# Eleven weight blocks that a matrix engine read as plain FP32 are split in two halves, and one tile's searches move

## The chip, the cores and the metric

The kernel runs on one core of a Trainium2 chip. The core has a matrix engine (TensorE, in the profile PE, with PEld for its weight loads), three engines for elementwise work (VectorE or DVE, ScalarE or ACT, GpSimd or POOL) and SyncE (SP), which issues most of the DMA transfers. Each engine executes its own list of instructions in order, and waits on semaphores for the others. The metric is the device time of one execution in microseconds; lower is better.

## The reference, cut to what matters

One layer of a streaming encoder on 512 tokens of width 1024: a normed and modulated mixer (short convolution and a gated linear recurrence), and then a retrieval layer over 16384 single-neuron experts. Nearly all of the time is in the retrieval, and the change is there:

```python
h = modulate(rmsnorm(x, norm2_g[l]), sh2, sc2)
x = x + g2[:, None, :] * peer(h, w_q[l], sub_keys[l], expert_u[l], expert_v[l])
...
q = (xb @ w_q).reshape(p, PEER_HEADS, 2, PEER_DK_HALF)
sc = jnp.einsum('phcd,hcnd->phcn', q, sub_keys)          # two rows of 128 scores per head
top_s, top_i = lax.top_k(sc, PEER_TOPK)                  # 16 best of each
cand_s = (top_s[:, :, 0, :, None] + top_s[:, :, 1, None, :]).reshape(p, PEER_HEADS, kk)
best_s, best_pos = lax.top_k(cand_s, PEER_TOPK)          # 16 best of 256 pairs
idx = jnp.take_along_axis(cand_i, best_pos, axis=-1)
g = jax.nn.softmax(best_s, axis=-1)
act = jax.nn.gelu(jnp.einsum('phkd,pd->phk', expert_u[idx], xb), approximate=False)
return jnp.einsum('phk,phkd->pd', g * act, expert_v[idx])
```

## The kernel before, in words

The tokens stand in four tiles of 128. For the first tile and for 64 tokens of the second the kernel gathers the experts' rows and takes products token by token (the sparse way: 192 products with rows of `expert_u`, called dots, 128 weighted sums with rows of `expert_v`; GpSimd issues a gather of 512 KB for each). For the other 320 tokens it computes all 16384 activations as matrix products, in 128 blocks of 128 experts (the dense way).

In order of time: the adaLN vectors, the mixer, its output projection; then

- **the norm stretch** (205 to 235 us): the second norm. For each of eight slices of the width VectorE scales, ScalarE writes the upper part of the modulated input (L364), VectorE the rest of it (L365). The upper and lower parts `h2h` and `h2l` together carry the FP32 value. L674 writes it a third time, unsplit, to `h2f`, for the 320 dense tokens.
- **the query phase** (to 279 us): for each of eight heads one block of `w_q` is split and multiplied, transposed queries are copied (`qT`, L728), multiplied by the keys, and the scores are copied to `sc` (L738). VectorE searches the scores meanwhile. One step of the search (`top16`, L690 to L699) takes one head and one tile of tokens: the best eight of each of two rows of 128, their places, a copy without them, and the next eight. The generator `early` lists the steps that are done here, `HQ` heads with four tiles each. At its end the activations of block 0 are computed (L740).
- **the activation phase** (to about 770 us): blocks 1 to 123 of activations, with the weights streamed from HBM. `w_load` starts the load of a block, `w_high` lets ScalarE write the upper part of the weights (`whi`, L74) and `w_low` lets VectorE write the rest (`wlo`, L79). A split block takes 24 matmuls (`mm3`, L88 to L90): upper by upper, upper by lower, lower by upper. ScalarE then evicts the block through a gelu (L1150).
- **the second phase** (to about 1310 us): the dense products with `expert_v`, 18 matmuls of 128x512 for each of 128 blocks (L1349), the other activation blocks, the sums of the sparse way (L1083), and the output.

Blocks 1 to 11 are an exception in the kernel before (`k < FN`, FN = 12). They aren't split: their raw FP32 weights are multiplied by `h2f` in eight FP32 matmuls (L1159), of two records each in the trace. From block 5 on the raw weights are loaded to the buffers of `whi` and `wlo`; those of blocks 1 to 4 to `wraw`. Each of the three rings has four buffers.

What sets the order around the change: in the query phase the order of the program and a scheduler that places each engine's instructions; from block 0 on an order written by the loop at L1278. For each block k it issues the low half of block k+2, the matmuls, and the high half of block k+3, and then lets generators hand out VectorE's other work: `searches_E` (the rest of the searches that the second tile needs, then its final top 16 and positions in `topk_tile`), `rest_E` (the remaining searches), `gates_E` (the dense gates), `dots`. How much is handed out for a block is counted in nanoseconds by `pe`, `dve` and `ac`: a block adds its estimated TensorE time to `pe`, and VectorE's work is issued until `dve` has caught up. As soon as the second tile's positions are known (`idx_b`, L835), GpSimd's gathers open (L1045).

Names in the profile: `ps_act` and `ps_z` are sums in PSUM, `act` evicted activations, `h` the split input, `rows` gathered rows, `oh` one-hot or pair tables, `cl` and `ch` the split coefficients of the second phase. `in_uT_dram` and `in_v_dram` are the weights.

Of the kernel before, what the change touches and what calls it, by code (L numbers as in the profile page):

```python
# [34 lines left out]
def block_kernel(ctx, tc, xT, small, w_ada1, w_ada, b_ada, w_in, w_r, w_i, w_out, w_q, keys, uT, u, v, final_g, out):  # L35
# [618 lines left out]
    h2f = [ring.tile([128, 2, NU], F32, name="act", bufs=RB // 2) for _ in range(KB // 2)]  # L654
# [12 lines left out]
    for k in range(KB):  # L667
        if k == 2:
            qsp[1] = split_w(qraw[1])
            norm2.close()  # L670
        t1 = sq_pool.tile([128, T], F32, name="mt1")
        nc.vector.tensor_mul(t1, xs[:, k, :], psr2)
        modulate(t1, k, A2, adac[:, 24:32], h2h, h2l, full2)
        nc.scalar.activation(h2f[k // 2][:, k % 2], t1[:, T - NU:], AF.Identity, scale=A2[:, k:k + 1],  # L674
                             bias=adac[:, 24 + k:25 + k])
        if k < len(x1p):
            x1_out(*x1p[k])
# [30 lines left out]

    early = chain(*(stage1([h], range(NT)) for h in range(HQ)))

# [68 lines left out]
    def topk_tile(t):  # L779
# [30 lines left out]
        for w in range(2):  # L810
# [5 lines left out]
            if t == 1 and w == 0:  # L816
                yield None
# [146 lines left out]
    def searches_E():  # L964
        heads = range(HQ, 8)
        yield from stage1(heads, [1])
# [133 lines left out]
    def w_load(k):  # L1100
        if k < len(jobs):
            kind, i = jobs[k]
            if 5 <= k < FN:
                raw = wring.tile([128, KB, 128], FR, name=("wlo", "whi")[k % 2], bufs=WB).bitcast(F32)
                nc.sync.dma_start(raw, uT[i])
                wraw[k] = raw
                return
# [8 lines left out]
    def w_high(k):  # L1116
        if FN <= k < len(jobs):
            whi[k] = high(wraw[k])

    def w_low(k):  # L1120
        if FN <= k < len(jobs):
            wlo[k] = low(wraw.pop(k), whi[k])
            settle()
# [28 lines left out]
    def u_chunk(k, pool):  # L1152
        c = jobs[k][1]
        if c:
            ps = pool.tile([128, NU], F32, name="ps_act", bufs=3 if pool is psE else 2)
            if k < FN:
                raw = wraw.pop(k)
                for j in range(KB):
                    nc.tensor.matmul(ps, raw[:, j, :], h2f[j // 2][:, j % 2], start=j == 0, stop=j == KB - 1)  # L1159
            else:  # L1160
                mm3(ps, whi.pop(k), wlo.pop(k), hd, ld, range(KB), True, True)
# [5 lines left out]
        pe[0] += FPE if c and k < FN else 3530  # L1167
        dve[0] += 0 if c and k < FN - 2 else 1140
        ac[0] += 450 if c and k < FN - 3 else 1400
# [75 lines left out]
    pe, dve, ac = [0], [-HEAD], [0]  # L1245
# [32 lines left out]
    for k in range(CE):  # L1278
# [13 lines left out]
        dve[0] = max(dve[0], RHO * pe[0] - LEAD - (HEAD if k < 9 else 0))  # L1292
# [157 lines left out]
FN = 12  # L1450
DX = 0.3
FPE = 4400
# [6 lines left out]
HEAD = 0  # L1459
# [15 lines left out]
HQ = 5  # L1475
# [49 lines left out]
```

## Time and profile before

| | |
|---|---|
| median of 3 runs | 1326.58 us (1324.27 to 1328.68) |
| the profiled execution | 1323.76 us |
| its span on the core | 1321.9 us |
| TensorE busy | 1302.3 us |
| VectorE busy | 1209.9 us |
| ScalarE busy | 729.0 us |
| GpSimd busy | 505.8 us |
| mean DMA rate | 333 GB/s |

The profiled execution lies at the lower end of the three runs. A row of the timeline gives start, duration, engine, line, operation, what it writes and reads, how many instructions it joins, and in brackets the idle time ahead of it with what ended that. A row of a group of instructions gives busy time, the mean of one in ns, and the idle time ahead. A row of a stretch gives start and end, then TensorE, weight loads, VectorE, ScalarE and GpSimd with busy us and number of instructions, the granted TensorE clock, the DMA engines' busy share, and GB/s.

### The profile page before, as it was taken

How to read it: one execution, taken by the hardware profiler on the slowest of the kernel's cores; microseconds unless marked ns; L12 is line 12 of the kernel's file. 1: busy time of each engine (PE TensorE's matmuls, PEld its weight loads, DVE VectorE, ACT ScalarE, POOL GpSimd, SP SyncE). 2: the span in 40 equal slices, each digit the busy share in tenths (PEclk: the TensorE clock that was granted, in tenths of full speed). 3: DMA queues.
4: the chain of work that ended last, by engine and by line, in shares of the span. 5: the costliest groups of instructions: out<-in, count | busy, mean ns of one | idle time of the engine just before them, and what ended most of it. 6: DMA issues, size and time to landing. Idle time of an engine off the chain costs nothing.

```text
span 1321.9 us, 21365 instructions
## 1 busy us (share of the span) xinstructions
PE 1302.3 (99%) x7506; PEld 1127.4 (85%) x7506; DVE 1209.9 (92%) x2241; ACT 729.0 (55%) x1319; POOL 505.8 (38%) x342
## 2 busy tenths in 40 slices
PE   8999999999999999999999999999999999999996
PEld 6677777777999999999999998888888888888884
DVE  6889975899999999999999679999899999999998
ACT  4577736424785987799679543334343434343433
POOL 0000002300253126324655545677556555455560
PEclk9999999999999999999999999999999999999998
DMA  9765542342899999999999999999999999999993
GB/s 373 268 245 175 182 137 96 117 153 75 297 377 353 318 343 399 418 357 341 417 408 416 401 354 381 413 413 416 412 415 413 414 413 415 412 414 412 407 394 153
DMA packets 151276, 440.06 MB, mean 333 GB/s; under 512 B 17024, under 2 KB 44672, under 8 KB 151168
## 3 DMA queue, kind: packets, MB, share of 16 engines
q1 hardware_dynamic: 104016, 267.23, 54.3%
q0 software_dynamic: 46864, 170.41, 32.4%
q8 instruction: 59, 0.97, 0.3%
q10 hardware_dynamic: 288, 1.05, 0.2%
q14 instruction: 49, 0.40, 0.1%
HBM read 393.54 MB, written 45.09 MB: 332 GB/s over the span
## 4 chain that ended last, share of the span: by engine, by line
PE 74%; DMA 12%; DVE 9%; issue 3%; ACT 1%; DVEq 0%; SPq 0%; ACTq 0%
PE acc L1349 19%; PE ps_act L88 10%; PE ps_act L90 10%; PE ps_act L89 10%; DMA wraw<-in_v_dram 9%; PE ps_z L89 4%; PE ps_z L90 4%; PE ps_z L88 4%; PE ps_act L1159 4%; PE ps_gt L908 3%; DVE ys L1083 2%; DMA h<-Gd 2%; DVE wlo L79 1%; PE ps_z L346 1%; DMA raw<-in_v_dram 1%
## 5 line engine op out<-in xcount | busy, mean ns | idle before, releaser
L74 ACT ACTIVATE whi<-wraw 128x1024 fp32r<-128x1024 f32 x255 | 270.6, 1062 | 263.4 <-DMA wraw<-in_v_dram 176.0
L79 DVE TENSOR_TENSOR wlo<-wraw,whi 128x1024 fp32r<-128x1024 f32 x249 | 303.4, 1219 | 33.7 <-ACT whi L74 33.3
L88 PE MATMUL ps_act<-h,whi 128*128 128x320 f32 x928 | 291.8, 314 | 0.0
L89 PE MATMUL ps_act<-h,whi 128*128 128x320 f32 x928 | 287.1, 309 | 0.0
L90 PE MATMUL ps_act<-h,wlo 128*128 128x320 f32 x928 | 287.1, 309 | 0.0
L1045 POOL DMA_INDIRECT rows<-in_u_dram,idx_s x128 | 200.3, 1565 | 152.7 <-DVE scr L1066 106.5
L1045 POOL DMA_INDIRECT rows<-in_v_dram,idx_s x128 | 191.0, 1492 | 156.9 <-DVE ys L1083 134.9
L1349 PE MATMUL acc<-whi,cl 128*128 128x512 f32 x744 | 229.4, 390 | 0.0
L1349 PE MATMUL acc<-wlo,ch 128*128 128x512 f32 x744 | 229.3, 389 | 0.0
L1349 PE MATMUL acc<-whi,ch 128*128 128x512 f32 x744 | 229.2, 389 | 0.0
L1045 POOL DMA_INDIRECT rows<-in_u_dram,idx_b x64 | 94.0, 1469 | 212.2 <-DVE scr L1066 151.5
L88 PEld LDWEIGHTS ps_act<-h,whi 128*128 128x128 f32 x928 | 174.3, 188 | 0.5
L89 PEld LDWEIGHTS ps_act<-h,whi 128*128 128x128 f32 x928 | 174.5, 188 | 0.2
L90 PEld LDWEIGHTS ps_act<-h,wlo 128*128 128x128 f32 x928 | 174.3, 188 | 0.0
L1066 DVE SCALAR_TENSOR_TENSOR scr<-rows,h2n 128x1024 f16<-128x1024 f32 x128 | 156.4, 1222 | 12.3 <-DMA rows<-in_u_dram,idx_s 10.8
L1083 DVE SCALAR_TENSOR_TENSOR ys<-rows,acts,ys 128x1024 f32<-128x1024 f32 x127 | 163.6, 1288 | 1.5
L1349 PEld LDWEIGHTS acc<-whi,cl 128*128 128x128 f32 x744 | 139.6, 188 | 29.3 <-DVE cl L1240 0.3
L1349 PEld LDWEIGHTS acc<-wlo,ch 128*128 128x128 f32 x744 | 139.7, 188 | 29.0
L1349 PEld LDWEIGHTS acc<-whi,ch 128*128 128x128 f32 x744 | 139.5, 188 | 28.5
L1150 ACT ACTIVATE act<-ps_act 128x320 f32<-128x320 f32 x127 | 56.5, 445 | 108.3 <-PE ps_act L90 75.4
L896 ACT ACTIVATE igh<-oh,gl 128x128 f16<-128x128 f16 x320 | 99.6, 435 | 0.6 <-DVE oh L875 0.4
L595 POOL DMA_DIRECT2D x1d<-xn x8 | 4.6, 582 | 214.6 <-ACT xn L594 212.5
(326 smaller groups left out, 1933.1 us busy)
## 6 DMA issues: line engine op xcount, KB each, us to landing
wraw<-in_uT_dram SPq DMA_DIRECT2D x120, 512.0 KB, 7.2
wraw<-in_v_dram SPq DMA_DIRECT2D x103, 512.0 KB, 14.1
Gd<-stg SPq DMA_DIRECT2D x46, 512.0 KB, 8.9
wada<-in_w_ada_dram SPq DMA_DIRECT2D x45, 512.0 KB, 6.1
Ad<-act SPq DMA_DIRECT2D x48, 320.0 KB, 7.7
act<-Ad SPq DMA_DIRECT2D x48, 320.0 KB, 14.6
raw<-in_v_dram SPq DMA_DIRECT2D x25, 512.0 KB, 13.8
h<-Gd SPq DMA_DIRECT2D x48, 256.0 KB, 14.6
```

What stands on the lines that cost most here:

```text
L74: nc.scalar.activation(hi, raw, AF.Copy)
L79: (eng or nc.vector).tensor_sub(lo, raw, hi.bitcast(F32))
L88: nc.tensor.matmul(ps, hi[:, k, :], xh(k), start=first and k == ks[0], stop=False)
L89: nc.tensor.matmul(ps, hi[:, k, :], xl(k), start=False, stop=False)
L90: nc.tensor.matmul(ps, lo[:, k, :], xh(k), start=False, stop=last and k == ks[-1])
L896: nc.scalar.activation(ig[:, 1, k // 2, :, k % 2], of[:, k // 2, 0, :, k % 2], AF.Copy, scale=gl[:, t0 + k:t0 + k + 1])
L1045: nc.gpsimd.indirect_dma_start(out=r[:, :], out_offset=None, in_=table, in_offset=bass.IndirectOffsetOnAxis(ap=idxs[:, k:k + 1], axis=0))
L1066: nc.vector.scalar_tensor_tensor(scr, rows.pop(n), 1.0, hn, op0=OP.mult, op1=OP.mult, accum_out=dst[:, k:k + 1])
L1083: nc.vector.scalar_tensor_tensor(ys, rows.pop(k), acts[:, k:k + 1], ys, op0=OP.mult, op1=OP.add)
L1150: nc.scalar.activation(act[c // 2][:, c % 2], ps, AF.Gelu)
L1159: nc.tensor.matmul(ps, raw[:, j, :], h2f[j // 2][:, j % 2], start=j == 0, stop=j == KB - 1)
L1349: nc.tensor.matmul(accs[b][e], st[:, bs], mv[:, e * 512:(e + 1) * 512], start=first, stop=last)
```

## The change

`h2f` and L674 go. Blocks 1 to 11 are split like all others: `w_load` reads them to `wraw`, `w_high` splits every block, and `w_low` gives the low halves of blocks below PL = 10 to GpSimd, those of 10 and 11 to VectorE. The counters take 3530 ns for every block, and VectorE's counter adds nothing for blocks whose low half (two blocks ahead) is GpSimd's. `HQ` is 4 instead of 5, and `early` gets the second tile's (tile 1) searches of heads 4, 5 and 6 in addition: 16 + 3 = 19 steps instead of 20. Only head 7 of the second tile is left to `searches_E` (one step instead of three), and `rest_E` has twelve steps instead of nine. In `topk_tile` the second tile's second copy of positions is issued one block later.

```diff
-    h2f = [ring.tile([128, 2, NU], F32, name="act", bufs=RB // 2) for _ in range(KB // 2)]
...
         modulate(t1, k, A2, adac[:, 24:32], h2h, h2l, full2)
-        nc.scalar.activation(h2f[k // 2][:, k % 2], t1[:, T - NU:], AF.Identity, scale=A2[:, k:k + 1],
-                             bias=adac[:, 24 + k:25 + k])
...
-    early = chain(*(stage1([h], range(NT)) for h in range(HQ)))
+    early = chain(*(stage1([h], range(NT)) for h in range(HQ)), stage1(range(HQ, 7), [1]))
...
             yield None
-            if t == 1 and w == 0:
+            if t == 1:
                 yield None
...
     def searches_E():
-        heads = range(HQ, 8)
-        yield from stage1(heads, [1])
+        yield from stage1([7], [1])
...
-            if 5 <= k < FN:
-                raw = wring.tile([128, KB, 128], FR, name=("wlo", "whi")[k % 2], bufs=WB).bitcast(F32)
-                nc.sync.dma_start(raw, uT[i])
-                wraw[k] = raw
-                return
...
     def w_high(k):
-        if FN <= k < len(jobs):
+        if k < len(jobs):
             whi[k] = high(wraw[k])
 
     def w_low(k):
-        if FN <= k < len(jobs):
-            wlo[k] = low(wraw.pop(k), whi[k])
+        if k < len(jobs):
+            wlo[k] = low(wraw.pop(k), whi[k], nc.gpsimd if k < PL else None)
             settle()
...
-            if k < FN:
-                raw = wraw.pop(k)
-                for j in range(KB):
-                    nc.tensor.matmul(ps, raw[:, j, :], h2f[j // 2][:, j % 2], start=j == 0, stop=j == KB - 1)
-            else:
-                mm3(ps, whi.pop(k), wlo.pop(k), hd, ld, range(KB), True, True)
+            mm3(ps, whi.pop(k), wlo.pop(k), hd, ld, range(KB), True, True)
...
-        pe[0] += FPE if c and k < FN else 3530
-        dve[0] += 0 if c and k < FN - 2 else 1140
-        ac[0] += 450 if c and k < FN - 3 else 1400
+        pe[0] += 3530
+        dve[0] += 0 if k < PL - 2 else 1140
+        ac[0] += 1400
...
-        dve[0] = max(dve[0], RHO * pe[0] - LEAD - (HEAD if k < 9 else 0))
+        dve[0] = max(dve[0], RHO * pe[0] - LEAD)
...
-FN = 12
+PL = 10
...
-HQ = 5
+HQ = 4
```

The change moves instructions on every engine. On GpSimd, from the mixer's last copies to the sparse gathers, before (an operation with a count is that many in a row):

```order
L595 DMA x1d<-xn 128x512 x8
L79 TENSOR_TENSOR wlo<-wraw,whi 128x1024 x6
L766 MEMSET ssum 128x8
L767 DMA rows<-in_u_dram,ssum 128x1024
L1045 DMA rows<-in_u_dram,idx_b 128x1024 x64
```

and now:

```order
L595 DMA x1d<-xn 128x512 x8
L79 TENSOR_TENSOR wlo<-wraw,whi 128x1024 x10
L763 MEMSET ssum 128x8
L764 DMA rows<-in_u_dram,ssum 128x1024
L79 TENSOR_TENSOR wlo<-wraw,whi 128x1024 x5
L1041 DMA rows<-in_u_dram,idx_b 128x1024 x64
```

Six low halves (of `w_q` blocks) become ten, with blocks 1 to 4 of the activations, and five more (blocks 5 to 9) stand between the first gather, which fetches nothing that is used, and the sparse ones.

On ScalarE, at the end of the query phase, before:

```order
L728 ACTIVATE qT<-ps_z 128x512
L738 ACTIVATE sc<-ps_g 128x512 x2
L728 ACTIVATE qT<-ps_z 128x512
L740 ACT_TABLE_LOAD
L740 ACTIVATE act<-ps_z 128x320
L738 ACTIVATE sc<-ps_g 128x512 x2
L1150 ACTIVATE act<-ps_act 128x320 x5
```

and now:

```order
L725 ACTIVATE qT<-ps_z 128x512
L74 ACTIVATE whi<-wraw 128x1024
L737 ACT_TABLE_LOAD
L737 ACTIVATE act<-ps_z 128x320
L735 ACTIVATE sc<-ps_g 128x512 x2
L1141 ACTIVATE act<-ps_act 128x320
L74 ACTIVATE whi<-wraw 128x1024
```

The last head's scores (`sc`, the last such row in both) now stand behind the high half of block 4, and a high half stands between any two evictions.

On VectorE, before, around the first two low halves after the query phase (blocks 12 and 13; `oh` with `tif` is the second position's comparison, `ij` its result):

```order
L697 MAX top<-rep 128x8 x2
L699 MAX_INDEX ti<-top,rep 128x8 x2
L79 TENSOR_TENSOR wlo<-wraw,whi 128x1024
L824 TENSOR_TENSOR oh<-oh,io_2727 128x2048
L825 TENSOR_TENSOR oh<-oh,tif 128x2048
L828 TENSOR_TENSOR oh<-oh 128x128x8
L828 TENSOR_TENSOR oh<-oh 128x128x4
L828 TENSOR_TENSOR oh<-oh 128x128x2
L829 TENSOR_TENSOR ij<-oh 128x128
L79 TENSOR_TENSOR wlo<-wraw,whi 128x1024
```

and now, where the three low halves are those of blocks 11, 12 and 13, and the one of block 10 is one search step further ahead:

```order
L79 TENSOR_TENSOR wlo<-wraw,whi 128x1024
L694 MAX top<-rep 128x8 x2
L696 MAX_INDEX ti<-top,rep 128x8 x2
L687 MAX top<-sc 128x8 x2
L689 MAX_INDEX ti<-top,sc 128x8 x2
L691 MATCH_REPLACE rep<-top,sc 128x128 x2
L79 TENSOR_TENSOR wlo<-wraw,whi 128x1024
L821 TENSOR_TENSOR oh<-oh,io_2703 128x2048
L822 TENSOR_TENSOR oh<-oh,tif 128x2048
L79 TENSOR_TENSOR wlo<-wraw,whi 128x1024
L825 TENSOR_TENSOR oh<-oh 128x128x8
L825 TENSOR_TENSOR oh<-oh 128x128x4
```

Block 12's low half now stands in the middle of a search step, and block 13's inside the second position's comparison, ahead of the sums that it followed before.

More of the change, by code (lines that the diff above doesn't have):

```diff
@@ L1244, in block_kernel @@
     dot_gen = gens["d"]
-    pe, dve, ac = [0], [-HEAD], [0]
+    pe, dve, ac = [0], [0], [0]
     late_k = {}
@@ L1449 @@
 GPE = 460
-FN = 12
+PL = 10
 DX = 0.3
-FPE = 4400
 SE = 0.65
@@ L1458 @@
 KG = 4
-HEAD = 0
 NS = 56000
```

## The prediction

> **What bounds the kernel now.** I read the page first, then TensorE's waits over the two phases that stream weights, then the busy times stretch by stretch, and last the rows on either side of the blocks that change. The profiled execution took 1323.76 us and its span is 1321.9.
>
> ```profile
> PE 1302.3 (99%) x7506; PEld 1127.4 (85%) x7506; DVE 1209.9 (92%) x2241; ACT 729.0 (55%) x1319; POOL 505.8 (38%) x342
> PE   8999999999999999999999999999999999999996
> ```
>
> TensorE is busy 99% of the span, and only the first and the last of forty slices are below nine tenths. A busy digit does not exclude short waits, so these are the rows of TensorE's waits from 280 to 1290 us (total, times, longest):
>
> ```profile
> PE acc L1342 <- DVE cl L1240: 1.7, 1, 1.7
> PE ps_gt L908 <- DVE igh L889: 0.5, 1, 0.5
> ```
>
> In 1010 us TensorE waits 2.2 us for anybody. So a microsecond of matrix work taken out is a microsecond gained, as long as what feeds TensorE keeps up. Who feeds it shows in the stretches (TensorE, weight loads, VectorE, ScalarE, GpSimd, clock, DMA share, GB/s):
>
> ```profile
> 205.00:235.00 30.00, 28.92 (x178) 21.09 (x176) 18.23 (x33) 22.82 (x37) 8.67 (x10) 1.00 0.34 123
> 279.00:327.00 48.00, 48.00 (x186) 34.01 (x183) 47.59 (x294) 14.76 (x20) 1.12 (x2) 1.00 0.35 116
> 327.00:360.00 33.00, 32.54 (x251) 32.07 (x251) 32.58 (x122) 23.03 (x56) 7.18 (x5) 1.00 0.74 257
> 360.00:560.00 200.00, 200.00 (x1589) 197.55 (x1588) 196.31 (x383) 159.67 (x353) 76.89 (x53) 1.00 0.98 368
> 560.00:785.00 225.00, 224.94 (x1704) 220.48 (x1703) 198.94 (x279) 167.00 (x387) 103.89 (x68) 1.00 1.00 386
> 785.00:1290.00 505.00, 505.00 (x2251) 419.69 (x2250) 476.51 (x514) 196.67 (x252) 297.29 (x196) 1.00 1.03 409
> ```
>
> The second row is the stretch of blocks 1 to 11. VectorE is as full there as TensorE (47.59 of 48), while ScalarE, GpSimd and the DMA (0.35) have room. Until 560 us VectorE has only 0.4 and 3.7 us to spare in a stretch; from there it has 26.1 and then 28.5, and the DMA is the full one.
>
> **Blocks 1 to 11 on TensorE.** The chain and ScalarE's evictions price a block before and after:
>
> ```profile
> 279.41 47.57 PE ps_act L1159 x176
> 288.25 0.44 ACT L1150 ACTIVATE act<-ps_act 128x320 f32<-128x320 f32 x1 [3.87 <-PE ps_act L1159]
> 292.56 0.44 ACT L1150 ACTIVATE act<-ps_act 128x320 f32<-128x320 f32 x1 [3.87 <-PE ps_act L1159]
> 398.25 0.44 ACT L1150 ACTIVATE act<-ps_act 128x320 f32<-128x320 f32 x1 [2.13 <-PE ps_act L90]
> 401.76 0.44 ACT L1150 ACTIVATE act<-ps_act 128x320 f32<-128x320 f32 x1 [0.34 <-PE ps_act L90]
> ```
>
> The 176 records are 16 for each of eleven blocks. Two evictions of plain blocks are 292.56 − 288.25 = 4.31 us apart, two of split blocks 401.76 − 398.25 = 3.51 (3.52 for others below). With 3.52 a block gains 0.79 and eleven gain **8.7 us**. The chain is on TensorE all the while, so all of it counts.
>
> **The norm stretch.** The eight plain copies of the normed input go from ScalarE:
>
> ```profile
> L674 ACT ACTIVATE act<-mt,adac,A 128x320 f32<-128x320 f32 x8 | 5.2, 644 | 0.0
> 216.04 0.50 PE L88 MATMUL ps_z<-h,whi 128*128 128x512 f32 x1 [0.71 <-ACT h L364]
> ```
>
> That is 5.2 us of ScalarE, but TensorE stands still only 30 − 28.92 = 1.1 us in the whole stretch, 0.71 of it for ScalarE. Bounds 0 and 1.1; I take **0.5**, a little under the one wait that ScalarE ends.
>
> **The halves that are new.** Eleven high halves on ScalarE cost nothing: it is busy 14.76 of 48 us there. Nine low halves on GpSimd and two on VectorE:
>
> ```profile
> 241.95 2.37 POOL L79 TENSOR_TENSOR wlo<-wraw,whi 128x1024 fp32r<-128x1024 f32 x1 [3.89 <-ACT whi L74]
> 242.25 0.46 DVE L690 MAX8 top<-sc 128x8 f32<-128x128 f32 x2
> 244.59 0.46 DVE L690 MAX8 top<-sc 128x8 f32<-128x128 f32 x2
> 322.83 1.20 DVE L79 TENSOR_TENSOR wlo<-wraw,whi 128x1024 fp32r<-128x1024 f32 x1
> 323.95 1.21 DVE L824 TENSOR_TENSOR oh<-oh,io 128x2048 f16<-128x2048 f16 x1
> 326.45 1.65 DVE L828 TENSOR_TENSOR oh<-oh 128x1024 f16<-128x1024 f16 x3
> 328.47 1.22 DVE L79 TENSOR_TENSOR wlo<-wraw,whi 128x1024 fp32r<-128x1024 f32 x1
> 332.55 1.22 DVE L79 TENSOR_TENSOR wlo<-wraw,whi 128x1024 fp32r<-128x1024 f32 x1
> 340.10 1.21 DVE L79 TENSOR_TENSOR wlo<-wraw,whi 128x1024 fp32r<-128x1024 f32 x1
> 327.01 0.44 ACT L1150 ACTIVATE act<-ps_act 128x320 f32<-128x320 f32 x1 [2.93 <-PE ps_act L1159]
> 330.52 0.44 ACT L1150 ACTIVATE act<-ps_act 128x320 f32<-128x320 f32 x1 [2.12 <-PE ps_act L90]
> 334.04 0.44 ACT L1150 ACTIVATE act<-ps_act 128x320 f32<-128x320 f32 x1 [2.14 <-PE ps_act L90]
> ```
>
> GpSimd needs 2.37 us for one against 3.52 that a block lasts, so it can follow. VectorE's four low halves are those of blocks 12, 13, 14 and 17. They end at 324.03, 329.69, 333.77 and 341.31; TensorE wants them when the block ahead ends, at 327.01, 330.52, 334.04 and (three blocks of 3.52 later) 344.6. Their leads are 3.0, 0.8, 0.3 and 3.3 us.
>
> All four must now come 8.7 us earlier. In the new order VectorE has less ahead of them: a search step takes 244.59 − 242.25 = 2.34, three and a half fewer stand ahead of block 12's low half (7.0, and 0.9 for the second part of a step, two of its five passes), and two low halves more (2 × 1.12 from start to next start): 5.7 less. Ahead of block 13's it is 5.7 + 2.0 = 7.7 less, because what ran from 326.45 to 328.47 now comes behind it. For 14 the same count over the new order gives 8.4, for 17 it gives 4.2. New leads: 3.0 + 5.7 − 8.7 = 0.0, then −0.2, 0.0 and −1.2. TensorE waits as long as the worst: **a = 1.2 us**. Bounds 0 (a late TensorE makes its own slack) and 8.7, if none of the shortening reaches VectorE.
>
> The two low halves more (2.2 us) are hidden later, as are the four dots that the new order leaves for the last phase, by the 26.1 us that VectorE idles from 560 to 785 and the 28.5 from there. With that cover gone 2.2 us and four dots would be paid.
>
> **Head 7's scores (b).** The moved searches make VectorE want the last table of scores after 19 steps rather than leave it for later, and in ScalarE's new order block 4's high half and the table load stand ahead of it:
>
> ```profile
> L74 ACT ACTIVATE whi<-wraw 128x1024 fp32r<-128x1024 f32 x255 | 270.6, 1062 | 263.4 <-DMA wraw<-in_v_dram 176.0
> 275.51 1.28 ACT L740 ACT_TABLE_LOAD   x1
> 278.35 0.44 ACT L740 ACTIVATE act<-ps_z 128x320 f32<-128x320 f32 x1 [1.56 <-PE ps_z L90]
> 279.44 1.09 ACT L738 ACTIVATE sc<-ps_g 128x512 f32<-128x512 f32 x2 [0.65 <-PE ps_g L732]
> 279.63 0.46 DVE L690 MAX8 top<-sc 128x8 f32<-128x128 f32 x2
> ```
>
> Block 4's high half needs the buffer of block 0's, so it starts when block 0's matmuls end, 278.35. Then 1.06 for it, 1.28, 0.44 and 1.09: the scores land at 282.2. VectorE's twentieth step started at 279.63. So it loses at most 2.6 us, and nothing if its other work covers that: eight small set-up instructions now stand ahead of that step. I take the middle, **b = 1.3**. Behind that step on VectorE stand the second tile's positions and block 10's low half, so a loss here arrives whole at blocks 10 to 17, whose leads are already gone.
>
> **GpSimd beside VectorE (c).** The low half at 241.95 ran under search steps that kept their 2.34, so these do not mind. Operations with two inputs from SBUF are another matter:
>
> ```profile
> 331.85 0.94 POOL L1045 DMA_INDIRECT rows<-in_u_dram,idx_b  x1 [0.30 <-issue]
> 334.60 2.34 DVE L79 TENSOR_TENSOR wlo<-wraw,whi 128x1024 fp32r<-128x1024 f32 x2
> 334.88 2.87 POOL L1045 DMA_INDIRECT rows<-in_u_dram,idx_b  x1 [0.30 <-issue]
> L824 DVE TENSOR_TENSOR oh<-oh,st 128x2048 f16<-128x2048 f16 x1 | 1.2, 1227 | 0.0
> ```
>
> An issue on GpSimd took 2.87 instead of 0.94 while VectorE subtracted: here GpSimd was the one that waited. The low halves of blocks 5 to 9 now fall into the time of two VectorE clusters of such operations (the pair sums, and the first position's comparison of the last row). Bounds: nothing, and a whole GpSimd subtraction each, 2 × 2.37 = 4.7. I take half a subtraction in half of the meetings, **c = 1.2**. The Trainium skill ("SBUF — State Buffer", section "Who interferes with whom") states that a VectorE instruction with two SBUF inputs and a GpSimd one that reads SBUF shut each other out, the later one blocking entirely, and that one-input instructions do not contend; the undisturbed search steps agree, and by that rule every meeting that GpSimd enters first would cost VectorE, and the time would be that of the rival *VectorE late* below.
>
> **What costs nothing.** The later second copy has the remaining searches to cover it; uncovered it would cost one block, 3.5 us. The gathers that need the positions come 4.5 us earlier by my count of VectorE's work, into a stretch with a DMA share of 0.35. The loads are the same bytes on the same queue, and GpSimd's five late low halves stand only ahead of gathers that wait for those positions anyway.
>
> **Sum:** 1323.8 − 8.7 − 0.5 + 1.2 + 1.3 + 1.2 = 1318.3. The profiled execution is 2.8 us below the median of the three runs (1326.6), so the median to expect is **1321.1**, its own range 1317.5 to 1324.
>
> **Rivals.**
>
> *Nothing waits:* a, b and c are nothing and the norm stretch gives all 1.1. 1323.8 − 9.8 + 2.8 = 1316.8. Against it: four leads that I find at or below zero.
>
> *VectorE late:* b and c at their upper bounds, 1.2 + 2.6 + 4.7 = 8.5, give 1323.8 − 9.2 + 8.5 + 2.8 = 1325.9. For it: 47.59 of 48 us busy. Against it: the row where GpSimd was the one to wait. It decides if TensorE waits over 5 us between 280 and 315.
>
> *The last phase is the DMA's:* TensorE comes 5 us sooner to a stretch whose DMA share is 1.03, and four gathers more are left for it.
>
> ```profile
> ACT whi L74 <- DMA wraw<-in_v_dram: 173.6, 74, 5.1
> wraw<-in_v_dram SPq DMA_DIRECT2D x103, 512.0 KB, 14.1
> ```
>
> ScalarE waits 173.6 us there for weights that take 14.1 us to land. Four gathers of 0.524 MB at 0.409 MB/us are 5.1 us: 1321.1 + 5.1 = 1326.2. Against it: TensorE has no DMA wait there in before.
>
> *Slower, GpSimd keeps VectorE out:* each of the five subtractions of blocks 5 to 9 holds VectorE for its 2.37 us, since VectorE's work is chained and it cannot take another instruction first. 11.9 + 1.2 + 1.3 = 14.4, and 1323.8 − 9.2 + 14.4 + 2.8 = 1331.8. It makes the kernel slower from the point where VectorE's slip by block 17 passes 9.2 us. Against it: the search steps, most of VectorE's work there, have one input.
>
> **How the numbers follow.** Forecast 0.45, nothing waits 0.08, VectorE late 0.20, DMA 0.15, slower 0.12. About 0.3%, 4 us, is what can be told from no change: faster is below 1322.6, slower above 1330.6. Four fifths of the forecast (0.36), the first rival and a fifth of the next two (0.07) give faster 0.51; the last rival is slower, 0.12; the rest is same, 0.37. The range 1315 to 1328.5 holds all but the last rival and the tails.
>
> **What would show it.** Evictions of blocks 1 to 11 3.52 us apart show the main term. Waits of TensorE for low halves between 280 and 345 us are a + b + c: near 3.7 the forecast, near 0 the first rival, 8 and more the others. GpSimd's low halves longer than 2.4, or VectorE's comparison longer than 1.23, show who pays for c. New waits of TensorE for weights after 785 show the DMA rival. The forecast is wrong if the evictions stay 4.3 apart or if TensorE's total wait from 280 to 785 exceeds 9.

## The result, and the profile after

The changed kernel takes **1334.08 us** (median of 9 runs, 1330.11 to 1337.81) against 1324.27 for the kernel before (median of 9 as well): a ratio of 1.0079, 95% interval 1.0066 to 1.0091. It is 10 us slower, where 1321.1 was forecast. The profiled execution took 1335.67 us with a span of 1333.6.

Two lines of the page, the busy times and the slices of TensorE's clock:

```profile
PE 1304.2 (98%) x7594; PEld 1139.1 (85%) x7594; DVE 1219.8 (91%) x2243; ACT 735.6 (55%) x1322; POOL 532.2 (40%) x351
PEclk9999999998999999999999999999999999999998
```

TensorE's four longest waits from 200 to 1310 us (total, times, longest):

```profile
PE ps_act L90 <- DVE wlo L79: 5.9, 1, 5.9
PE acc L1328 <- DVE cl L1226: 2.9, 1, 2.9
PE ps_gt L905 <- ACT igh L893: 2.3, 1, 2.3
PE acc L1335 <- DVE cl L1226: 0.8, 2, 0.5
```

TensorE's busy time says little: it rose by 2 us although the eleven blocks got shorter, in part because time at a lower clock counts as busy. The waits say more. One of 5.9 us stands in the stretch of the changed blocks, one of 2.3 at 641 us, one at the very end. The first shows in the timeline with its clock. Four short stretches around it (start and end, TensorE, weight loads, VectorE, ScalarE, GpSimd, clock, DMA share, GB/s):

```profile
313.00:316.00 3.00, 0.11 (x1) 0.00 (x0) 2.93 (x18) 1.88 (x2) 0.00 (x0) 1.00 0.07 26
319.00:321.00 2.00, 1.96 (x7) 1.96 (x8) 2.00 (x15) 0.00 (x0) 0.00 (x0) 0.50 0.48 98
321.00:323.00 2.00, 2.00 (x10) 2.00 (x9) 2.00 (x8) 0.00 (x0) 0.00 (x0) 0.50 0.41 164
325.00:327.00 2.00, 2.00 (x16) 2.00 (x15) 2.00 (x2) 1.31 (x2) 0.00 (x0) 1.00 0.73 291
```

After standing still from 313 to 319 TensorE works at half its clock until about 324 us. Measured against the usual start-to-start times of its matmuls, the stretch from 300 to 340 us is about 8.9 us too long, 6.1 for the wait and 2.8 for the clock. The 8.7 us that the eleven blocks save are gone right there: counted from the end of block 0 in each execution, block 11 is evicted 0.2 us later than before. The Trainium skill ("TensorE: Matmul & The Clock Gate", section "What's actually happening") says that an idle window of about 3.4 us sets the clock to half and a busy one releases it; the rows agree.

What had the wait come from? VectorE's rows and, below, GpSimd's beside them, in the same execution:

```profile
281.04 2.11 DVE L751 TENSOR_SCALAR rep<-iota 128x16 f32<-128x16 f32 x1
286.85 2.21 DVE L781 TENSOR_TENSOR oh<-top 128x128 f32<-128x128 f32 x4
296.72 2.38 DVE L798 SCALAR_TENSOR_TENSOR msk<-pos,msk 128x128 uint32<-128x128 uint32 x1
317.78 1.21 DVE L79 TENSOR_TENSOR wlo<-wraw,whi 128x1024 fp32r<-128x1024 f32 x1
```

```profile
280.66 2.41 POOL L79 TENSOR_TENSOR wlo<-wraw,whi 128x1024 fp32r<-128x1024 f32 x1 [1.18 <-ACT whi L74]
285.90 2.40 POOL L79 TENSOR_TENSOR wlo<-wraw,whi 128x1024 fp32r<-128x1024 f32 x1 [1.49 <-ACT whi L74]
296.45 2.49 POOL L79 TENSOR_TENSOR wlo<-wraw,whi 128x1024 fp32r<-128x1024 f32 x1 [1.12 <-ACT whi L74]
```

Each of the three VectorE rows ahead of the low half begins while GpSimd subtracts, and ends after GpSimd does: GpSimd's end at 283.07, 288.30 and 298.94, VectorE's rows at 283.15, 289.06 and 299.10. In the kernel before, with no subtraction of GpSimd beside them, the same three rows were:

```profile
281.96 0.15 DVE L754 TENSOR_SCALAR rep<-iota 128x16 f32<-128x16 f32 x1
289.76 0.87 DVE L784 TENSOR_TENSOR oh<-top 128x128 f32<-128x128 f32 x4
298.30 0.29 DVE L801 SCALAR_TENSOR_TENSOR msk<-pos,msk 128x128 uint32<-128x128 uint32 x1
```

That is 2.0 + 1.3 + 2.1 = 5.4 us. Block 10's low half ends at 318.99, and TensorE wanted it at about 313.

The rest of the loss is elsewhere. Here are two stretches of the activation phase and the second phase, of before and then of after:

```profile
450.00:560.00 110.00, 110.00 (x891) 108.47 (x891) 107.87 (x201) 88.83 (x209) 42.83 (x31) 1.00 0.99 380
560.00:660.00 100.00, 100.00 (x796) 98.75 (x795) 95.07 (x138) 83.46 (x185) 43.95 (x28) 1.00 0.98 372
```

```profile
450.00:560.00 110.00, 110.00 (x901) 108.30 (x900) 108.00 (x214) 99.53 (x224) 27.52 (x20) 1.00 0.93 330
560.00:660.00 100.00, 97.55 (x767) 95.08 (x766) 95.51 (x130) 78.63 (x185) 52.74 (x33) 0.98 1.02 402
785.00:1290.00 505.00, 504.15 (x2246) 417.87 (x2245) 477.70 (x520) 196.12 (x250) 305.52 (x198) 1.00 1.03 410
```

From 450 to 560 us VectorE is as full as before (108 of 110), but the DMA carries 330 GB/s instead of 380. VectorE does other things than dots there, and the gathers wait for the dots to free their buffers. The dots done by 560 us, before and after (64 of the first kind and then the others make 192):

```profile
L1066 DVE SCALAR_TENSOR_TENSOR scr<-rows,h2b 128x1024 f16<-128x1024 f32 x53 | 64.7, 1221 | 0.4
```

```profile
L1062 DVE SCALAR_TENSOR_TENSOR scr<-rows,h2b 128x1024 f16<-128x1024 f32 x42 | 51.2, 1219 | 0.2
```

Eleven gathers are put off. They come in a burst afterwards (1.02 of the DMA from 560 to 660), weights come late in it, and that is the wait at 641 us. ScalarE stands still 5.0 us for weights there, and the table (`igh`) that TensorE waits for comes right behind:

```profile
641.85 1.06 ACT L74 ACTIVATE whi<-wraw 128x1024 fp32r<-128x1024 f32 x1 [5.00 <-DMA wraw<-in_uT_dram]
642.82 2.48 ACT L893 ACTIVATE igh<-oh,gl 128x128 f16<-128x128 f16 x8
```

Block 123, the last of the phase, is evicted at these times, before and after:

```profile
772.38 0.44 ACT L1150 ACTIVATE act<-ps_act 128x320 f32<-128x320 f32 x1 [1.40 <-PE ps_act L90]
```

```profile
777.81 0.44 ACT L1141 ACTIVATE act<-ps_act 128x320 f32<-128x320 f32 x1 [1.41 <-PE ps_act L90]
```

So the activation phase ends 5.4 us later with 111 dots done instead of 115, and the second phase, whose DMA is full from 785 to 1290 us (1.03), takes another 6.3 us longer: 11.7 us in the span. Not all of the 5.4 is the change's. This execution was 1.4 us behind at its matmuls of 20 us already, ahead of everything that the change touches, and 1.3 us behind at the last matmul of block 0 (279.28 instead of 278.01). Another version of the changed kernel (run 2) was 0.6 us ahead at both places, so about 4 us of the 5.4 come from the change.

### The profile page after: what moved, and what is told of

The parts are those of the page before. It is cut to its first block, busy times and chain, and to the rows that moved or that the text cites. A ratio compares the mean times of both kernels' runs of the same rounds, so it can differ in the third digit from the quotient of the medians.

```text
span 1333.6 us, 21558 instructions
## 1 busy us (share of the span) xinstructions
PE 1304.2 (98%) x7594; PEld 1139.1 (85%) x7594; DVE 1219.8 (91%) x2243; ACT 735.6 (55%) x1322; POOL 532.2 (40%) x351
## 4 chain that ended last, share of the span: by engine, by line
PE 42%; DMA 27%; DVE 18%; issue 9%; ACT 2%; POOL 1%; DVEq 0%; SPq 0%; POOLq 0%; ACTq 0%
DMA wraw<-in_v_dram 9%; PE ps_act L88 7%; PE ps_act L90 7%; PE ps_act L89 7%; PE acc L1335 5%; DMA h<-Gd 4%; DMA rows<-in_u_dram,idx_s 4%; PE ps_z L89 3%; PE ps_z L88 3%; PE ps_z L90 3%; DVE scr L1062 2%; DVE wlo L79 2%; DMA raw<-in_v_dram 2%; PE ps_gt L905 2%; DMA gt<-Gd 2%
## 5 line engine op out<-in xcount | busy, mean ns | idle before, releaser
L74 ACT ACTIVATE whi<-wraw 128x1024 fp32r<-128x1024 f32 x266 | 281.1, 1058 | 239.2 <-DMA wraw<-in_v_dram 152.9
L79 DVE TENSOR_TENSOR wlo<-wraw,whi 128x1024 fp32r<-128x1024 f32 x251 | 307.4, 1225 | 38.9 <-ACT whi L74 38.6
L90 PE MATMUL ps_act<-h,wlo 128*128 128x320 f32 x1016 | 316.1, 311 | 5.9 <-DVE wlo L79 5.9
L88 PE MATMUL ps_act<-h,whi 128*128 128x320 f32 x1016 | 320.7, 316 | 0.0
L89 PE MATMUL ps_act<-h,whi 128*128 128x320 f32 x1016 | 316.0, 311 | 0.0
L1041 POOL DMA_INDIRECT rows<-in_v_dram,idx_s x128 | 195.5, 1527 | 147.4 <-DVE ys L1079 125.2
L90 PEld LDWEIGHTS ps_act<-h,wlo 128*128 128x128 f32 x1016 | 192.3, 189 | 6.2 <-DVE wlo L79 6.2
L88 PEld LDWEIGHTS ps_act<-h,whi 128*128 128x128 f32 x1016 | 192.4, 189 | 0.8 <-ACT act L1141 0.3
L89 PEld LDWEIGHTS ps_act<-h,whi 128*128 128x128 f32 x1016 | 192.4, 189 | 0.2
```

Of the source, the lines that this page charges most:

```text
L74: nc.scalar.activation(hi, raw, AF.Copy)
L79: (eng or nc.vector).tensor_sub(lo, raw, hi.bitcast(F32))
L88: nc.tensor.matmul(ps, hi[:, k, :], xh(k), start=first and k == ks[0], stop=False)
L89: nc.tensor.matmul(ps, hi[:, k, :], xl(k), start=False, stop=False)
L90: nc.tensor.matmul(ps, lo[:, k, :], xh(k), start=False, stop=last and k == ks[-1])
L1041: nc.gpsimd.indirect_dma_start(out=r[:, :], out_offset=None, in_=table, in_offset=bass.IndirectOffsetOnAxis(ap=idxs[:, k:k + 1], axis=0))
```

## The experiments

Ratios are against the kernel before, run beside each version on the same chip; its medians there were 1323.4 to 1323.9 us. The first theory was that VectorE's lateness at block 10, with what the clock adds, is most of the loss. It fell after the first four runs.

**1. Low halves of blocks 5 to 9 on VectorE.**

```diff
-            wlo[k] = low(wraw.pop(k), whi[k], nc.gpsimd if k < PL else None)
+            wlo[k] = low(wraw.pop(k), whi[k], nc.gpsimd if k < 5 else None)
```

> The changed kernel, but the low halves of blocks 5 to 9 go to VectorE instead of GpSimd (1 to 4 stay on GpSimd; the order's counters are untouched). Theory (GpSimd's subtractions held VectorE up, 5.4 us in three rows, and block 10's low half came late by that): the long set-up, pair-sum and mask rows (2.11, 2.21, 2.38 us) fall back to 0.2, 0.9 and 0.3, VectorE gets 5 x 1.15 = 5.7 us of subtractions instead, so block 10 is as late as before, TensorE's wait there is about 6 us and the time about that of the change, 1334 (1331 to 1337). Rival (VectorE was not held up, the new order alone makes block 10 late): the three rows stay short or long as they were, and 5.7 us come on top, with the clock 1340 or more.

Measured 1337.51 us, ratio 1.0093 (1.0062 to 1.0123). The groups of VectorE from 279 to 330 us:

```profile
L751 DVE TENSOR_SCALAR rep<-iota 128x16 f32<-128x16 f32 x1 | 2.1, 2108 | 0.0
L781 DVE TENSOR_TENSOR oh<-top 128x128 f32<-128x128 f32 (+2 forms) x4 | 0.9, 284 | 0.0
L798 DVE SCALAR_TENSOR_TENSOR msk<-pos,msk 128x128 uint32<-128x128 uint32 x1 | 0.3, 293 | 0.0
```

The two rows that had met low halves of blocks 5 to 9 are short again; the first, which meets block 4's, is still 2.1. So GpSimd's subtractions lengthen them. But moving the five to VectorE costs as much as it frees: TensorE's waits for low halves come to 6.7 us in five pieces instead of 5.9 in one. The time is half a microsecond above the theory's window.

**2. VectorE's counter starts at 6000.**

```diff
-    pe, dve, ac = [0], [0], [0]
+    pe, dve, ac = [0], [6000], [0]
```

> The changed kernel, but VectorE's counter starts at 6000 ns, so about 7 us of searches and comparisons stand behind block 10's low half instead of ahead of it. Theory (lateness of VectorE at block 10, 6.1 us of wait and 2.8 us of lost clock behind it, is most of the loss): the wait between 305 and 330 us falls below 1 us, the clock stays at 1.00 there, and the time falls by about 8.9 to 1325 (1322 to 1328), near the kernel before. Rival (the loss is in later phases, waits for gates at 641 us and in the second phase): under 3 us gained, 1331 or more.

Measured 1333.04 us, ratio 1.0064 (1.0045 to 1.0082). The stretch of the wait, and the second phase:

```profile
309.00:327.00 18.00, 18.00 (x125) 18.00 (x124) 17.86 (x67) 8.73 (x11) 0.00 (x0) 1.00 0.59 182
785.00:1290.00 505.00, 500.48 (x2211) 411.73 (x2210) 478.65 (x523) 193.33 (x246) 313.80 (x201) 1.00 1.03 411
```

The wait is gone, the clock is full, and block 13 is evicted 9.3 us earlier than in the kernel before, 8.7 of them counted from the end of block 0: the saving that the prediction counted, complete. Yet the whole gains 1 us. Block 123 is evicted at 768.14, still 4.2 us ahead of before, but with 105 dots done instead of 115. In the second phase TensorE then waits nine times for split coefficients, and the span ends 8.6 us late. This run ended the first theory: the wait at block 10 is real, and taking it away only moves the loss.

**3. Low halves up to block 17 on GpSimd.**

```diff
+            wlo[k] = low(wraw.pop(k), whi[k], nc.gpsimd if k < 18 else None)
```

> The changed kernel, but the low halves of blocks 10 to 17 go to GpSimd too (the counters stay as they were, so the rest of VectorE's order does not move). Theory: block 10's low half no longer stands behind VectorE's work, TensorE's wait there goes (at most 2 us left, if later subtractions meet VectorE's comparisons), and the first low half on VectorE, block 18, has about 3 us of lead: 1325 (1321 to 1329). Rival (GpSimd's subtractions hold VectorE up wherever they are, and VectorE is what TensorE waits for): eight more of them cost VectorE another 5 us and more, the first low half on VectorE comes late as block 10 did, 1332 or more.

Measured 1334.30 us, ratio 1.0075 (1.0055 to 1.0095). TensorE's waits from 300 to 345 us:

```profile
PE ps_act L88 <- ACT act L1141: 2.5, 1, 2.5
PE ps_act L90 <- POOL wlo L79: 2.3, 1, 2.3
PE ps_t L848 <- DVE g L838: 1.3, 1, 1.3
```

Three shorter waits replace the long one: ScalarE stuck behind a copy that waits for VectorE, GpSimd itself, and VectorE. The reason stands in VectorE's rows, the comparison that took 1.20, 1.23 and 1.61 us in the changed kernel:

```profile
307.56 2.94 DVE L821 TENSOR_TENSOR oh<-oh,st 128x2048 f16<-128x2048 f16 x1
310.53 3.32 DVE L822 TENSOR_TENSOR oh<-oh,dif 128x2048 f16<-128x2048 f16 x1
313.89 3.72 DVE L825 TENSOR_TENSOR oh<-oh 128x1024 f16<-128x1024 f16 x3
```

Beside four subtractions of GpSimd (304.62 to 316.12) they cost VectorE 5.9 us more. So the rival's number came, and its first half as well; its late block 18 did not.

**4. The split alone**, with the searches as before.

```diff
-    early = chain(*(stage1([h], range(NT)) for h in range(HQ)), stage1(range(HQ, 7), [1]))
+    early = chain(*(stage1([h], range(NT)) for h in range(HQ)))
...
-HQ = 4
+HQ = 5
```

> The changed kernel with the searches as before (20 steps in the query phase, heads 5 to 7 of the second tile behind it, the second copy not delayed): the split of blocks 1 to 11 alone. Theory (every microsecond of VectorE ahead of block 10 counts): one search step more, 2.3 us, stands ahead of block 10, so TensorE's wait there is about 8 us, the time 1336 to 1339. Rival (the moved searches are themselves what made it slower): the time falls to the kernel before or below it, 1325 or less.

Measured 1329.09 us, ratio 1.0041 (1.0026 to 1.0057): between the two expectations. The moved searches account for about half of the loss, and the theory's step more ahead of block 10 did not make it worse: the low halves fell on other VectorE rows there, and the wait was 4.6 us.

The four runs suggested another theory: **the second phase is the DMA's, the activation phase VectorE's, and TensorE, though busy 99%, bounds neither.** Runs 11 and 12 will correct its last part. The next four runs change the kernel before by one dose each, a little work taken out or put in at one place.

**5. Less TensorE work in the kernel before.**

```diff
-                mm3(ps, whi.pop(k), wlo.pop(k), hd, ld, range(KB), True, True)
+                if 60 <= k < 68:
+                    hi, lo = whi.pop(k), wlo.pop(k)
+                    for j in range(KB):
+                        nc.tensor.matmul(ps, hi[:, j, :], hd(j), start=j == 0, stop=False)
+                        nc.tensor.matmul(ps, lo[:, j, :], hd(j), start=False, stop=j == KB - 1)
+                else:
+                    mm3(ps, whi.pop(k), wlo.pop(k), hd, ld, range(KB), True, True)
```

> The kernel before, with the upper-by-lower product left out in activation blocks 60 to 67 (64 matmuls of 0.147 us, 9.4 us of TensorE; those blocks' activations lose that term). If TensorE is what bounds the kernel before, as the prediction had it: 1323.4 - 9.4 = 1314. If the last phase is paced by the DMA, whose bytes are the same: the last phase starts up to 9.4 us earlier and ends within 3 us of before, 1320.5 to 1323.4, with new waits of TensorE in it.

Measured 1323.22 us, ratio 0.9996 (0.9987 to 1.0006). Nothing of 9.4 us arrives. The stretch of those blocks, and then TensorE's longest wait in it:

```profile
520.00:560.00 40.00, 35.44 (x263) 32.77 (x262) 39.97 (x95) 27.01 (x62) 17.93 (x14) 0.96 1.03 417
```

```profile
PE ps_gt L908 <- ACT igh L896: 3.4, 1, 3.4
```

TensorE spends the time waiting, already here and not only in the second phase as I had expected: VectorE (39.97 of 40) and the DMA (1.03) are both full in it, and this run doesn't tell which of the two held it. Against the usual start-to-start times of TensorE's matmuls the stretch is 8.9 us too long, waits and lower clock together, so the relief is used up right there; block 123 is evicted 1.0 us earlier than before.

**6. More DMA in the second phase of the kernel before.**

```diff
+            if n in range(34, 98, 2):
+                nc.sync.dma_start(dummy, v[n * 128:(n + 1) * 128, 0:256])
```

> The kernel before, with 32 loads of 128 KB in the second phase that nobody uses (4.2 MB, to one spare tile). If the DMA paces the second phase, at the 0.41 MB/us of its windows: 4.2 / 0.41 = 10.2 us longer, 1333.6. If TensorE or VectorE does, and the transfers are hidden: within 2 us of before, 1323 to 1326.

Measured 1336.86 us, ratio 1.0093 (1.0074 to 1.0112): 13.4 us longer, somewhat more than the bytes alone. TensorE's waits from 785 us on, which in the kernel before are one of 1.7:

```profile
PE acc L1349 <- DVE cl L1240: 6.5, 14, 1.4
PE acc L1342 <- DVE cl L1240: 2.9, 1, 2.9
```

The name after the arrow is VectorE, but the dose was the DMA's. The waits of ScalarE and VectorE in the second phase of the same run show the way between:

```profile
ACT whi L74 <- DMA wraw<-in_v_dram: 198.9, 81, 5.6
DVE wlo L79 <- ACT whi L74: 36.0, 33, 2.6
```

ScalarE waits for weights 198.9 us instead of 173.6, VectorE for ScalarE's high halves 36.0 instead of 22.3, and the coefficients `cl` stand behind those low halves in VectorE's order.

**7. More VectorE work in the second phase.**

```diff
+            if n in range(34, 98, 2):
+                nc.vector.tensor_sub(dummy, h2b[:, 0:256], h2n[:, 0:256])
```

> The kernel before, with 32 subtractions of 128x256 on VectorE in the second phase that nobody uses (about 0.29 us each, 9.3 us). If VectorE paces the second phase: up to 9 us longer, 1330 or more. If the DMA does: VectorE has 28 us of idle time there, within 2 us of before, 1323 to 1326.

Measured 1323.01 us, ratio 0.9997 (0.9984 to 1.0009). The subtractions were longer than expected, 0.417 us each. Their group, from 800 to 1200 us:

```profile
L1392 DVE TENSOR_TENSOR dummy<-h2b,h2n 128x256 f32<-128x256 f32 x32 | 13.4, 417 | 0.0
```

So 13.4 us of VectorE cost nothing. In the second phase more DMA costs its full price, and more of VectorE, which TensorE's waits name, does not.

**8. The gates' deadline, in the kernel before.**

```diff
-KG = 4
+KG = -4
```

> The kernel before, with the deadline of the dense gates moved by eight blocks (KG -4 instead of 4), so that VectorE's order has more dots early: 61 instead of 59 ahead of block 78's low half, 117 instead of 115 by the end of the activation phase. If each gathered row that is left for the second phase costs its transfer (0.524 MB, 1.27 us): two fewer, 2.5 us faster, 1321. If the end does not depend on it: 1323 to 1324.

Measured 1322.70 us, ratio 0.9995 (0.9986 to 1.0004): no difference that can be told. The two dots more are VectorE work that the activation phase must hold; it ended 0.55 us later.

**9 and 10. The same deadline in the changed kernel and in the split alone.**

> The changed kernel with the deadline of the dense gates moved by eight blocks (KG -4 instead of 4): its dots come about as densely again as before the change (38 instead of 31 ahead of block 62's low half, 56 instead of 50 for block 78, 112 instead of 111 at the end; the kernel before has 41, 59 and 115). Theory (the DMA paces the kernel from about 450 us on; what the change lost is the wait at block 10 and the gathers that its order puts off): TensorE's wait at 641 us goes, since no burst of gathers meets the weights, and three instead of four gathers are left over: 5.3 and 1.3 us less, 1327.5 (1325.5 to 1330). If the order of the dots has nothing to do with it: 1334.

> The split alone (searches as before) with the dense gates' deadline moved by eight blocks: 114 dots by the end of the activation phase, one fewer than before, and 58 ahead of block 78. Theory: the activation phase ended 0.5 us ahead of before in the split alone, 2.6 us without the wait that came with its burst of gathers; one gather more left over is 1.3 us. So 1.3 us faster than before, 1322 (1320 to 1325). If the order of the dots has nothing to do with it: 1329, as the split alone.

Measured 1328.56 us, ratio 1.0044 (1.0028 to 1.006), and 1325.00 us, ratio 1.0013 (1.0002 to 1.0024). Five and a half and four microseconds come back by putting the dots first, with no instruction more or fewer in what is computed. In the changed kernel the stretch from 450 to 560 us now reads

```profile
450.00:560.00 110.00, 109.60 (x887) 107.79 (x886) 107.85 (x208) 91.38 (x208) 41.45 (x27) 1.00 0.95 361
```

with 361 GB/s instead of 330, and TensorE's wait at 641 us is gone. The split alone keeps shorter waits (1.9 and 1.2 us for ScalarE), and stays 3 us above its expectation.

**11 and 12. The DMA out of the way.** In both the loads of every second block of the second phase's weights that goes to `wraw` are left out:

```diff
+            if kind == "v" and i % 2:
+                wraw[k] = h2n.rearrange("p (k e) -> p k e", k=KB)
+                return
```

> The kernel before, with the loads of every second block of the second phase's weights left out (about 51 of 128; the blocks are made from a tile that is in SBUF already, all else is computed). 27 MB or 65 us of transfers less. Theory: TensorE's work is not shortened, and it never waited there, so 1319 to 1323; this is the base for the run below.

> The changed kernel with VectorE's counter at 6000 ns and the same loads left out. Theory (the second phase is paced by the DMA, and with the DMA out of the way what TensorE saves shows at the end): the activation phase ends 4.2 us ahead of before, and so does the kernel: 3 to 6 us below the run above. If the loss lies with VectorE or TensorE in the second phase: as much above it as with all loads, 8 to 10 us.

Measured 1322.06 us (ratio 0.9990, 0.9981 to 0.9999) and 1318.80 us (ratio 0.9963, 0.9949 to 0.9978). The second phase of the two:

```profile
785.00:1290.00 505.00, 505.00 (x2252) 419.72 (x2251) 482.86 (x516) 189.88 (x251) 282.26 (x196) 1.00 0.96 361
```

```profile
785.00:1290.00 505.00, 504.98 (x2245) 419.03 (x2244) 492.22 (x534) 191.79 (x251) 312.53 (x203) 1.00 0.98 370
```

With all loads the changed kernel with late counter was 9.7 us slower than before; with a part of them left out it is 3.3 us faster than its base, 4.2 by the spans of the profiled executions. There its activation phase ends 4.3 us ahead of the base's, so the lead reaches the end. The kernel before gains only 1.8 us: there TensorE is the bound beside the DMA. From the first to the 2200th of the second phase's 2304 matmuls it takes 513.1 us with all loads and 512.9 with a part left out; the changed kernel takes 515.0, with the counter at 6000 it is 520.9. So the theory was wrong about TensorE. In the kernel before TensorE runs at its own pace and the DMA just keeps up: less of either gains next to nothing, and more DMA is paid for. No run added work to TensorE.

**13. More VectorE work in the activation phase of the kernel before.**

```diff
+        if 36 <= k < 68:
+            nc.vector.tensor_sub(rowp.tile([128, D], F16, name="scr")[:, 0:256], h2b[:, 0:256], h2n[:, 0:256])
```

> The kernel before, with 32 subtractions on VectorE beside activation blocks 36 to 67 (about 425 to 555 us) that nobody uses; in the second phase such a subtraction took 0.417 us, so 13.4 us in all. If VectorE paces the activation phase there (it was busy 196 of 200 us) and TensorE's saving only met that: TensorE waits for it and the end comes 8 to 13 us later, 1331 to 1337. If TensorE paces it and VectorE's leads absorb this: within 2 us of before, 1322 to 1326.

Measured 1333.22 us, ratio 1.0071 (1.0054 to 1.0089). The subtractions, and TensorE's wait from 420 to 600 us:

```profile
L1282 DVE TENSOR_TENSOR scr<-h2b,h2n 128x256 f16<-128x256 f32 x32 | 13.3, 417 | 0.0
```

```profile
PE ps_gt L908 <- DVE igh L889: 5.5, 2, 3.5
```

The same 13.3 us that cost nothing in the second phase cost 9.6 here. Block 123 is 8.6 us late. VectorE has no room in this phase. Whether the DMA, at 0.98 there, has any was not tried.

**14. The moved searches alone.**

```diff
-    early = chain(*(stage1([h], range(NT)) for h in range(HQ)))
+    early = chain(*(stage1([h], range(NT)) for h in range(HQ)), stage1(range(HQ, 7), [1]))
...
-HQ = 5
+HQ = 4
```

> The kernel before with the moved searches and the later second copy alone (blocks 1 to 11 plain as before, no new work for GpSimd). The changed kernel was 5 us slower than the split alone. If the moved searches cost that by themselves: 1328. If they cost it only where GpSimd's subtractions and the missing leads meet them: their order has 117 instead of 115 dots by the end of the activation phase, which gained nothing measurable in the run with the moved deadline, so 1321 to 1324.

Measured 1327.91 us, ratio 1.0030 (1.0020 to 1.0040). They cost 4.2 us by themselves, and with the 5.7 of the split alone make up the change. 19 steps instead of 20 in the query phase leave one step (2.3 us) more to VectorE in the activation phase, and the order has two dots more in it (2.4 us): 4.8 us, and block 123 is 5.75 us late. My account had left this out, although it is in the diff.

**One formula for all.** If the activation phase ends d us later than in the kernel before, and n dots fewer are done by then, each is a gather of 0.524 MB in a phase whose DMA moves 0.41 MB/us: 1.27 us. The span should differ by d + 1.27 n. From each run's own trace, one execution of each (evictions of block 123, dots counted up to there, spans); how late an execution was before the change begins is in d and in the span alike:

| run | d | n | d + 1.27 n | span, measured |
|---|---|---|---|---|
| the change | +5.4 | 4 | 10.5 | +11.7 |
| low halves 5 to 9 on VectorE | +8.1 | 4 | 13.2 | +14.1 |
| counter at 6000 | −4.2 | 10 | 8.5 | +8.6 |
| low halves up to 17 on GpSimd | +2.9 | 4 | 8.0 | +9.0 |
| split alone | −0.5 | 4 | 4.6 | +5.2 |
| searches alone | +5.75 | −2 | 3.2 | +3.8 |
| change, deadline moved | +1.4 | 3 | 5.2 | +4.4 |
| split, deadline moved | +2.2 | 1 | 3.4 | +1.2 |
| before, deadline moved | +0.55 | −2 | −2.0 | −1.4 |
| VectorE work in the activation phase | +8.6 | 0 | 8.6 | +8.2 |
| VectorE work in the second phase | −1.0 | 0 | −1.0 | −1.2 |
| less TensorE work | −1.0 | 0 | −1.0 | −1.7 |

Eleven of twelve agree within 1.2 us, the split with the moved deadline within 2.2. The formula was made after these runs. It can't be carried to more gathers saved, since TensorE then sets the pace: the two kernels with two dots more, and run 11 with 52 loads fewer, all end 547.6 to 547.8 us after block 123, where the kernel before takes 549.5. The run with more DMA has its own bytes to add, and with loads left out the formula does not hold, as it should not: there the DMA no longer paces.

VectorE's account gives the sign and the rough size of d, counted from the end of block 0. For the change it is 5.4 us of contention, 2.4 for the low halves of blocks 10 and 11, 2.3 for the moved step, less 4 dots of 1.22 not done: 5.2, where 4.1 was measured. For the split alone, whose rows L781 and L798 lost 0.6 and 2.1 us, it gives 2.7 + 2.4 − 4.9 = 0.2 against 0.1, for the searches alone 4.8 against 5.8, for the counter at 6000, with ten dots fewer, −2.1 against −3.6. It does not fit the moved deadlines: for the change with it, 10.1 less three dots gives 6.4 where 1.6 was measured. There the order matters beside the sum, and I cannot say how. None of the versions beats the kernel before clearly; the best of the full computations, the kernel before with the moved deadline, is not to be told from it.

## Why the prediction was wrong, step by step

**"A microsecond of matrix work taken out is a microsecond gained."** This is the step that failed. 99% busy and 2.2 us of waits show that nobody is slower than TensorE, not that the others have room: VectorE at 196 of 200 us from 360 to 560 and the DMA at 1.03 from 785 to 1290 were just as full. The condition "as long as what feeds TensorE keeps up" stood in the text, and the rows that contradict it stood beside it. Run 5 took 9.4 us from TensorE and gained none, run 2 kept the whole 8.7 through block 13 and ended 9.7 us above the kernel before; only with the DMA relieved (run 12) did a part, 3.3 us, reach the end.

**The 8.7 us of the blocks.** Right as a size: without waits (run 2) block 13 came 8.7 us earlier, counted from the end of block 0. But alone it is not a term of the time.

**The norm stretch, 0.5.** From 210 to 250 us the distance to the kernel before shrank by 0.26 us. Small, as said, and TensorE's wait of 0.7 is still there.

**a, the low halves.** I listed blocks 12, 13, 14 and 17 as VectorE's, from the rows of before. That passed over 15 and 16, the two in a row at 334.60, and left out 10 and 11, which are new on VectorE and come first. TensorE waited for block 10, not 17. By the same count its lead would also have been about 0.

**b, head 7's scores, 1.3.** Nothing was waited for. The scores were in place at 283.3; the set-up ahead of the step, one row of it lengthened to 2.1 us by GpSimd, lasted until 284.5.

**c, GpSimd beside VectorE, 1.2 with bounds 0 and 4.7.** Mis-sized: 5.4 us, above the upper bound. I counted two meetings of blocks 5 to 9; a third came from block 4, with a one-input operation that I had taken to be safe like the search steps. I halved it twice on the strength of one row where GpSimd had waited. The Trainium skill's rule ("SBUF — State Buffer", section "Who interferes with whom") that the later one blocks entirely held in all three. What I gave as its word on one-input instructions lacked its exception, the modes that use both ports; the same section counts tensor_scalar among the operations that can enter one, which agrees with the 2.11. Another TENSOR_SCALAR (L797, 128x128 uint32) began 0.02 us behind the third subtraction and kept its 0.22, so which one-input operations wait stays open. My price for the rival stopped at the meetings I had listed.

**"What costs nothing."** The two low halves and the four dots were hidden, I wrote, by VectorE's idle 26 us from 560 on; that the moved search step comes back as work behind the query phase was no cost in any term (run 14: 4.2 us). Idle time later does not help work that is due earlier: until 560 VectorE had 4 us.

**The gathers.** I forecast the positions 4.5 us earlier. The first gather on them left at 333.5 instead of 330.6. Four dots fewer by the end of the phase was right, and 5.1 us for them as well: that rival, given 0.15, had the mechanism of the second phase and its size. It lacked that the activation phase would end late too.

**The base.** The 2.8 us that I added for the median came from three runs; over nine the kernel before has 1324.27, 0.5 above the profiled execution. The forecast in its own terms was 5.5 us faster, and it came 9.8 slower.

**The signs.** Evictions of the split blocks were 3.52 us apart, and TensorE's waits from 280 to 785 us were 5.9 + 2.3 = 8.2, under the 9 that I had set. So neither sign of being wrong showed: they count no time at a low clock, and they stop ahead of the phase where more than half of the loss fell.

**The slower rival, 1331.8**, had 0.12. Its time was near, and its place right; in its mechanism GpSimd holds VectorE five times, where it was three, and block 10 waits instead of 17. What it leaves out is the clock (2.8 us), the wait at 641 us and the gathers, so the nearness is partly luck.

## What to carry to other kernels

Taking work from an engine that is 99% busy pays only if the others have room; where two or three resources are full in a row of stretches, give the likely bound a dose (take a few microseconds away, add a few) before pricing a change by it. A change that relieves one of several full resources and adds even 2 us to another can lose: here most of VectorE's extra time in the activation phase came back as a late phase or as a gather that the DMA had to carry later. And when work moves to another engine, list the instructions that are new on each, in the new order, not only the old ones that shift.

## What the runs showed that I had not expected

- A one-input VectorE operation on 128x16 elements waited 2 us for GpSimd's subtraction (2.11 instead of 0.15), while search steps ran beside such subtractions at their usual length (2.3 us).
- The price of a wait of TensorE: after 5.9 us idle the clock was 0.50 for some 5 us and cost another 2.8; after the 2.3 us at 641, the ten microseconds from 640 had a mean clock of 0.83 and the excess was 5.3 in all.
- The same 13 us of VectorE work cost 9.6 us in one phase and nothing in the next.
- The engine after the arrow in TensorE's waits of the second phase is VectorE, though 13 us more of VectorE changed nothing there, and 4.2 MB more of DMA cost 13.4.
